# A Hymba-style encoder block: where four streams of elementwise work run, and in which order seven down products are taken

## The chip, the core and the metric

One NeuronCore of a Trainium2 chip runs the kernel. The metric is device time in microseconds, the median of several executions. Five engines have queues of their own, each of which works strictly in the order of the program: TensorE (PE, with its weight loads shown as PEld), VectorE (DVE), ScalarE (ACT), GpSimd (POOL) and SyncE (SP), which issues most of the DMAs. An engine that waits for a semaphore holds up everything behind it in its own queue.

## What is computed

Everything is float32. The input x has 512 rows (tokens) and 2048 columns.

```
h = rmsnorm(x, g_mix)
qA|kA|vA|qB|kB|vB = h @ w_in
out_a = rmsnorm(grouped attention of 8 heads over 2 key/value heads: q, k normalised per head, axial rotary)
out_b = rmsnorm(dilated window attention of 8 heads, partial rotary, three branches merged by softmax weight)
x = x + concat(out_a, out_b) @ w_out
gate, up = split(rmsnorm(x, g_ffn) @ w_gate_up)        # 2 x 5632 columns
x = x + (silu(gate) * up) @ w_down                      # 5632 x 2048
return rmsnorm(x, g_final)
```

## The kernel before

**Split operands.** A matmul here takes operands of a reduced float32 format (fp32r). To keep float32 accuracy each operand is a pair: `hi`, a copy rounded by ACT, and `lo`, the difference `src - hi` made by DVE. A product of two pairs is three matmuls (`mm3`, L133 to L135): hi·hi, hi·lo and lo·hi. So each weight tile of 128 x 1024 that arrives by DMA costs one ACT copy (`split_hi`, L223) and one DVE subtraction (`split_lo`, L231) before the twelve 128x512 matmuls that use it. One such tile with its matmuls is a unit (`Wides`). Its two pairs lie in one of four `twin` buffers.

**Seven products in place of eight.** The large projections use a Strassen-Winograd scheme: a 2x2 block product is made of seven products m1 to m7 of sums of blocks. The sums of weight blocks are made on DVE just before `split_hi` (`weights`, by `tt` at L297 in the projections and L1086 in down). In down (`class Down`, L1056) the weight block `a` of each of 22 row pairs is kept on chip in a `home` buffer. m1 uses a, m7 uses c - b. After that `between` (L1092 to L1095) adds c - b to `home` in place, and m6 (a itself), m4 (d - a) and m5 (c - a) read this new a; m2 uses d, m3 uses c. That in-place sum runs on GpSimd.

**Order of the units.** All units stand in one list that the last loop of the kernel walks. For unit n the loop loads weights some 20 us ahead (`load_raws`), makes `split_hi` up to three units ahead and `split_lo` up to two units ahead (`prepare`), emits the matmuls, runs hooks tied to that unit, and then takes small tasks from two queues `side` and `side2` (`pump`). A unit's `rate` is how many tasks of `side` it takes; `RATE_B`, `RATE_A` and `RATE_2` set this for the attention stage (in units with two halves, eight quarter-rate steps a unit). `drain_until` takes tasks at once where one is needed.

In down the order is written out: m1 leads and m7 follows 8 units behind (`LAG`), so 8 units of m1, then m1 and m7 in turns, then 8 units of m7 alone. Then the same with m6 and m4, and with m5 and m2, and at last m3 alone. m1, m6, m5 and m3 sum into the four PSUM banks called z; m7 and m4 into y, then m2 afresh into y. At the end of m1, m7, m6 and m4, `spill_out` (L1162) copies those four banks to `ev` buffers on ACT (L1167) and GpSimd's queue issues DMAs that add them into a DRAM tensor (L1168); one half of it behind the last unit, the other behind the next. The left operand, activations laid down in DRAM by the gate/up stage, comes in chunks of four row pairs (`chunk`, L1108): a DMA into `form_raw`, an ACT copy (L1119) and a DVE subtraction (L1123).

**The attention stage** runs as `side` tasks beneath the q projections of mixer A and the output projection. Each of 16 heads (`class Head`, L656) takes 12 tasks: transposes and splits of q and k, four `score` and four `weigh` tasks, and, one head later, `pt` (transposes of the probabilities with a split, L711, L124, L125) and `pv`. For a head of mixer B `score` takes the row maximum under a mask on DVE (L696) and at once issues the exponential on ACT (L698); `weigh` takes the reciprocal of its sum and scales the row.

**From attention to gate/up.** `h_side` (L933) turns the normalised rows and makes the block sums of the left operand; for the last column group its `lo` parts are made apart (L953), four of seven on DVE and three on GpSimd. The first gate/up block takes its 28 units in an order written out by hand (`first`, L973), since its last operands are made only then.

Of the kernel before, what the change touches and what calls it, by code (L numbers as in the profile page):

```python
# [14 lines left out]
AF = mybir.ActivationFunctionType  # L15
OP = mybir.AluOpType
# [31 lines left out]
PAIRS = NFF // 2  # L48
LAG = 8
TAIL = 4  # L50
CHUNK = 4
ORDER = ("m1", "m4", "m5", "m3", "m2", "m7", "m6")
X_AT = {"m1": (0, 1), "m4": (0, 2), "m2": (0, 3), "m5": (1, 0), "m6": (1, 1), "m7": (1, 2), "m3": (1, 3)}
RATE_B, RATE_A, RATE_2 = 3.2, 3.2, 3.2


def f32(ap):
    return ap.bitcast(F32)
# [3 lines left out]
def encoder_block(ctx, tc, x, w_in, g_q_a, g_k_a, w_out, w_gate_up, w_down, g_final,  # L62
                  c_xp, c_gain, c_ident, c_mask, c_axial, c_partial, out):
    nc = tc.nc
# [528 lines left out]
    def push_kvA():  # L593
        for t in range(NT):
            push_norm_rope(kvr["t"][:, t, :256], kvr["t"][:, t, :256], t, NKV, "k")

        def turn_k(kv):
            ps = bank("kt")
            for t in range(NT):
                nc.tensor.transpose(ps[:, t * P:(t + 1) * P], kvr["t"][:, t, kv * HD:(kv + 1) * HD], ident)  # L600
            kTA[kv] = split(ps, "kT", None, [kv_split[:, 2 * kv + n] for n in range(2)])

        def split_v():
            vA["v"] = split(kvr["t"][:, :, 256:], "vA", None, [kv_split[:, 4 + 2 * n:6 + 2 * n].rearrange(
                "p a (b c) -> p (a b) c", b=2) for n in range(2)])
        side2.extend((lambda: None, lambda: turn_k(0), split_v, lambda: turn_k(1)))

    q_rows = {}

    def post_qA(j, t, ps):  # L610
        if t == 0:
            q_rows[j] = slot("qA", F32, (P, NT, 512))
        q0 = q_rows[j][:, t]
        nc.scalar.activation(q0, ps[t], AF.Copy, scale=r1["r"][:, t:t + 1])
        push_norm_rope(q0, q0, t, 4, "q")
        side2.append(lambda: qA.__setitem__((j, t), q0))

# [38 lines left out]
    class Head:  # L656
# [27 lines left out]
        def score(self, t):  # L684
            if t == 0:
                self.negm, self.z, self.rz = small(), small(), small()
            ps = bank("sc")
            mm3(ps, cols(self.q, t * P), self.k, True, True)
            p = self.p[t] = slot("p")
            nmx, z = self.negm[:, t:t + 1], self.z[:, t:t + 1]  # L690
            if self.kind == "A":
                nc.vector.tensor_reduce(nmx, ps, axis=AX.X, op=OP.max, negate=True)
                nc.scalar.activation(p, ps, AF.Exp, bias=nmx, accum_out=z)
            else:
                lo = (NT - 1 - t) * P
                nc.vector.tensor_tensor_reduce(p, ps, mask[:, lo:lo + S], -1.0, 3e38, op0=OP.add, op1=OP.min,  # L696
                                               accum_out=nmx)
                nc.scalar.activation(p, p, AF.Exp, bias=nmx, scale=-1.0, accum_out=z)  # L698

        def weigh(self, t):  # L700
            p, rz = self.p[t], self.rz[:, t:t + 1]
# [58 lines left out]
    def push_heads():  # L760
        heads.extend([Head("B", h) for h in range(NHB)] + [Head("A", h) for h in range(NHA)])
        extra = {}
        for g in range(1, NHB // 2):
            h = 2 * g
            extra.setdefault((h - 2, 1), []).append(lambda g=g: load_pair_b(g))
            extra.setdefault((h - 1, 1), []).append(lambda g=g: rope_pair_b(g, "q"))
            extra.setdefault((h - 1, 3), []).append(lambda g=g: rope_pair_b(g, "k"))
            extra.setdefault((h, 1), []).append(lambda g=g: split_pair_v(g))

        def task(n, i):  # L770
            cur = heads[n] if n < len(heads) else None
            prev = heads[n - 1] if 0 < n <= len(heads) else None
            prev2 = heads[n - 2] if n > 1 else None
            t, first = i // 2 - 2, i % 2 == 0
            if t < 0:
                if first:
                    if cur:
                        (cur.tq, cur.tk)[i // 2]()
                else:
                    if prev and i == 1:  # L780
                        prev.weigh(3)
                    if prev2:
                        prev2.pv(2 + i // 2)
                        if i == 3:
                            prev2.fin()
            elif first:
                if prev:
                    if t > 1:
                        prev.pv(t - 2)
                    prev.pt(t)  # L790
            else:
                if cur:
                    cur.score(t)
                    if t:
                        cur.weigh(t - 1)
            for f in extra.get((n, i / 2), ()):
                f()
        for n in range(len(heads) + 1):
            side.extend(lambda n=n, i=i: task(n, i) for i in range(12))
        side.extend(lambda i=i: task(len(heads) + 1, i) for i in (1, 3))  # L800
# [44 lines left out]
    def out_chunk(kind, c):  # L845
# [21 lines left out]
        def post(t):  # L867
            drain_until(lambda: kind in ro, side2)
            nc.vector.scalar_tensor_tensor(x1[c][t], box[t], ro[kind][:, t:t + 1], x1[c][t], op0=OP.mult, op1=OP.add)
            if kind == "A" and c < NC - 1:  # L870
                square_x1(c, t)
            if t < NT - 1:
                return
            if kind == "B":
                hook(now[0] + 1, lambda: park_x1(c))
                return
            if c == 0:
                nc.scalar.activation(slot("table")[:, :1], ones, AF.Silu)
            if c == NC - 1:
                side.extend(lambda p=p: h_side(2 * c, p, True) for p in range(4))  # L880
                side.append(lambda: [square_x1(c, t) for t in (0, 1)])
                side.extend(lambda p=p: h_side(2 * c + 1, p, True) for p in range(2))
                side.append(lambda: park_x1(c))
                side.append(lambda: [square_x1(c, t) for t in (2, 3)])
                side.extend(lambda p=p: h_side(2 * c + 1, p, True) for p in range(2, 4))
                side.append(make_r2)
                return
            for i in (2 * c, 2 * c + 1):
                for part in range(3):
                    side.append(lambda i=i, part=part: h_side(i, part))  # L890
            side.append(lambda: park_x1(c))
# [41 lines left out]
    def h_side(i, half, apart=False):  # L933
# [12 lines left out]
        if half >= 2:  # L946
            for a, lo_part, n in ((0, 1, 4), (1, 5, 3)):
                src = hpart[0][:, lo_part:lo_part + n]
                hi, lo = (arena[a][:, :, i, j] for j in range(2))
                if half == 2:  # L950
                    nc.scalar.activation(hi, src, AF.Copy)
                if half == 3 or not apart:
                    (nc.gpsimd if apart and a else nc.vector).tensor_tensor(lo, src, f32(hi), op=OP.subtract)  # L953
        if half == (3 if apart else 2):
            hf[i] = True

# [13 lines left out]
    def gate_up_block(f0):  # L970
        first = None
        if f0 == 0:
            first = [("m1", 0), ("m1", 1), ("m1", 2), ("m2", 0), ("m2", 1), ("m7", 0), ("m7", 1), ("m1", 3), ("m7", 2),  # L973
                     ("m7", 3)] + [("m6", n) for n in range(4)] + [("m2", 2), ("m2", 3)] \
                + [(f, n) for f in ("m5", "m4", "m3") for n in range(4)]
        box = ColBlock(w_gate_up, 0, (f0 * P, DFF + f0 * P), KD // 4, form_of, 2, first, hf if f0 == 0 else None)
        if f0 == 0:
            for u in units[-len(first):][:10]:
                u.rate, u.load_ahead = 2.0, 10.0
        st = {}  # L980

# [74 lines left out]
    class Down:  # L1056
        BANK = {"m1": "z", "m6": "z", "m5": "z", "m3": "z", "m7": "y", "m4": "y", "m2": "y"}

        def __init__(self):
# [2 lines left out]
            self.home = [down_raw(0, 0, q, "home") for q in range(PAIRS)]  # L1062
            need = {"m1": "", "m7": "bc", "m6": "", "m4": "d", "m5": "c", "m2": "d", "m3": "c"}
            order = []
            for lead, lag in (("m1", "m7"), ("m6", "m4"), ("m5", "m2")):
                for q in range(PAIRS + LAG):
                    if q < PAIRS:
                        order.append((lead, q))
                    if q >= LAG:
                        order.append((lag, q - LAG))  # L1070
            order += [("m3", q) for q in range(PAIRS)]
            self.raws = {}
            for form, q in order:
# [18 lines left out]
        def between(self, form, q):  # L1092
            if form == "m7":
                a = self.home[q].t
                nc.gpsimd.tensor_tensor(a, self.raws[form, q]["b"].t, a, op=OP.add)  # L1095

        def chunks(self):
            uses = {}
# [63 lines left out]
    def spill_out(form, i, j):  # L1162
        def go(t):
            row = 2 * i + t
            for cb in range(2):
                e = evs[turns["ev"] % 2][:, cb]
                nc.scalar.activation(e, box.bank_of(form)[t][cb], AF.Copy, scale=r2["r"][:, row:row + 1])  # L1167
                nc.gpsimd.dma_start(x1_dram[2 * cb + j, row], e, accum_op=OP.add)  # L1168
            turns["ev"] += 1
        for t in range(2):  # L1170
            box.after(form, PAIRS - 1, t, lambda t=t: go(t))

    def add_in(ps, c, t, lo=0, hi=512):
        v = xd[c, t][:, lo:hi]
# [291 lines left out]
```

## Time and profile before

| what | value |
|---|---|
| median of 3 runs | 2009.89 us (2008.53 to 2010.05) |
| the profiled execution: its time / its span | 2010.6 us / 2008.5 us |
| granted TensorE clock, mean | 0.994 |
| busy over the span: PE, DVE, ACT, POOL | 1973.7, 1520.8, 994.2, 278.3 us |
| HBM read / written | 369.65 / 47.45 MB |

The 2.1 us between time and span lie outside the first and last instruction. PE's end times are modelled, so two matmuls that follow closely overlap in the record; the number of matmuls in a stretch tells more than its busy time. Rows of a timeline give start, duration, engine, line, operation, tiles written and read, shapes and count, and in brackets the idle time before and what ended it. Rows by stage give the stage's length, then busy time and number of instructions of PE, PEld, DVE, ACT and POOL, the granted clock, the DMA engines' share and GB/s.

### The profile page before, as it was taken

Reading aid. Unit: us, or ns where it says so; the run is one execution under the profiler, and the core shown is the slowest. Engines: PE = TensorE matmul, PEld = TensorE weight load, DVE = VectorE, ACT = ScalarE, POOL = GpSimd, SP = SyncE. Lnnn points to the kernel's source line nnn. Section 1 sums busy time; section 2 is a strip of 40 time slices with the busy share of each in tenths; the row PEclk is TensorE's granted clock in tenths of the full one; section 3 lists DMA queues with packets and bytes.
Section 4 is the critical chain, followed back from the end, with each engine's and each line's share of the span. In section 5 each row is a group of like instructions: output and inputs, shape, how many; then the busy total and the mean of one; then the engine's idle time right before and its main releaser. Section 6 shows DMA issues by size and latency. Waiting matters only on the chain.

```text
span 2008.5 us, 23826 instructions
## 1 busy us (share of the span) xinstructions
PE 1973.7 (98%) x8932; PEld 1622.4 (81%) x8932; DVE 1520.8 (76%) x1707; ACT 994.2 (49%) x1272; POOL 278.3 (14%) x261
## 2 busy tenths in 40 slices
PE   9999999999999999999999999999999997999998
PEld 7888888778888878888888888888888775888886
DVE  7777757877655687787787777777777999788776
ACT  7654445554435454444444444444544434455464
POOL 3100034663220000000000000000000355002000
PEclk9999999999999999999999999999999998999999
DMA  7777574242245664755856746747659976479855
GB/s 247 261 258 240 183 252 138 95 147 95 96 146 179 215 202 162 266 183 196 270 170 221 260 158 229 229 156 259 196 176 318 338 239 194 152 239 337 283 182 174
DMA packets 219091, 418.67 MB, mean 208 GB/s; under 512 B 13664, under 2 KB 40032, under 8 KB 218720
## 3 DMA queue, kind: packets, MB, share of 16 engines
q1 hardware_dynamic: 210176, 389.86, 58.2%
q0 software_dynamic: 8656, 27.27, 4.4%
q8 instruction: 70, 1.15, 0.2%
q14 instruction: 45, 0.37, 0.1%
q10 hardware_dynamic: 144, 0.02, 0.0%
HBM read 369.65 MB, written 47.45 MB: 208 GB/s over the span
## 4 chain that ended last, share of the span: by engine, by line
PE 89%; DVE 5%; issue 4%; ACT 2%; DMA 1%; POOL 0%; SPq 0%; ACTq 0%; POOLq 0%; DVEq 0%
PE zc L135 10%; PE zc L133 10%; PE zc L134 10%; PE yc L134 5%; PE yc L135 5%; PE yc L133 5%; PE zd L134 3%; PE zd L135 3%; PE zd L133 3%; PE pw L133 3%; PE pw L135 3%; PE pw L134 3%; PE xc L133 2%; PE xc L134 2%; PE xc L135 2%
## 5 line engine op out<-in xcount | busy, mean ns | idle before, releaser
L231 DVE TENSOR_TENSOR twin<-whole,twin 128x1024 fp32r<-128x1024 f32 x172 | 220.8, 1285 | 110.5 <-ACT twin L223 108.1
L223 ACT ACTIVATE twin<-st1b 128x1024 fp32r<-128x1024 f32 x172 | 182.6, 1062 | 214.8 <-PE zc L135 68.7
L133 PE MATMUL zc<-twin,arena 128*128 128x512 f32 x704 | 277.0, 394 | 0.0
L135 PE MATMUL zc<-twin,arena 128*128 128x512 f32 x704 | 274.7, 390 | 0.4 <-DVE arena L953 0.4
L134 PE MATMUL zc<-twin,arena 128*128 128x512 f32 x704 | 274.2, 389 | 0.0
L223 ACT ACTIVATE twin<-whole 128x1024 fp32r<-128x1024 f32 x172 | 181.6, 1057 | 157.5 <-PE yc L135 67.4
L231 DVE TENSOR_TENSOR twin<-st1b,twin 128x1024 fp32r<-128x1024 f32 x172 | 216.0, 1256 | 33.4 <-ACT twin L223 32.7
L223 ACT ACTIVATE twin<-st1a 128x1024 fp32r<-128x1024 f32 x128 | 135.8, 1061 | 192.8 <-PE xc L135 58.2
L231 DVE TENSOR_TENSOR twin<-st1a,twin 128x1024 fp32r<-128x1024 f32 x128 | 171.7, 1342 | 70.0 <-ACT twin L223 60.4
L135 PEld LDWEIGHTS zc<-twin,arena 128*128 128x128 f32 x704 | 132.1, 188 | 28.9 <-DVE arena L953 0.9
L133 PEld LDWEIGHTS zc<-twin,arena 128*128 128x128 f32 x704 | 132.2, 188 | 26.9
L134 PEld LDWEIGHTS zc<-twin,arena 128*128 128x128 f32 x704 | 132.3, 188 | 26.4
L1095 POOL TENSOR_TENSOR home<-st1a,home 128x1024 f32<-128x1024 f32 x8 | 24.5, 3102 | 869.4 <-DMA forms<-pair 855.3
L135 PE MATMUL zd<-twin,form 128*128 128x512 f32 x348 | 136.3, 392 | 5.2 <-DVE form L1123 5.2
L134 PE MATMUL yc<-twin,arena 128*128 128x512 f32 x352 | 137.2, 390 | 1.2 <-DVE twin L231 1.1
L133 PE MATMUL yc<-twin,arena 128*128 128x512 f32 x352 | 138.0, 392 | 0.0
L135 PE MATMUL yc<-twin,arena 128*128 128x512 f32 x352 | 137.2, 390 | 0.0
L134 PE MATMUL zd<-twin,form 128*128 128x512 f32 x348 | 136.0, 391 | 0.1
L133 PE MATMUL zd<-twin,form 128*128 128x512 f32 x348 | 135.9, 391 | 0.0
L134 PE MATMUL yd<-twin,form 128*128 128x512 f32 (+1 forms) x272 | 108.0, 397 | 9.9 <-DVE twin L231 9.9
L135 PE MATMUL yd<-twin,form 128*128 128x512 f32 (+1 forms) x272 | 107.5, 395 | 2.9 <-DVE form L1123 2.9
L133 PE MATMUL yd<-twin,form 128*128 128x512 f32 (+1 forms) x272 | 107.2, 394 | 0.0
(290 smaller groups left out, 4424.4 us busy)
## 6 DMA issues: line engine op xcount, KB each, us to landing
whole<-in_w_gate_up_dram SPq DMA_DIRECT2D x165, 512.0 KB, 5.8
whole<-in_w_in_dram SPq DMA_DIRECT2D x80, 512.0 KB, 4.5
st<-in_w_gate_up_dram SPq DMA_DIRECT2D x55, 512.0 KB, 3.9
st1a<-in_w_down_dram SPq DMA_DIRECT2D x48, 512.0 KB, 6.6
st1b<-in_w_down_dram SPq DMA_DIRECT2D x48, 512.0 KB, 7.5
st1a<-in_w_gate_up_dram SPq DMA_DIRECT2D x44, 512.0 KB, 7.7
st1b<-in_w_gate_up_dram SPq DMA_DIRECT2D x44, 512.0 KB, 7.3
forms<-pair SPq DMA_DIRECT2D x22, 896.0 KB, 6.4
```

Of the source, the lines that this page charges most:

```text
L133: nc.tensor.matmul(dst, ah, bh, start=start, stop=False, skip_group_check=chained)
L134: nc.tensor.matmul(dst, ah, bl, start=False, stop=False, skip_group_check=chained)
L135: nc.tensor.matmul(dst, al, bh, start=False, stop=stop, skip_group_check=chained)
L223: nc.scalar.activation(self.pair[:, :, 0], self.src, AF.Copy)
L231: nc.vector.tensor_tensor(self.pair[:, :, 1], self.src, f32(self.pair[:, :, 0]), op=OP.subtract)
L1095: nc.gpsimd.tensor_tensor(a, self.raws[form, q]["b"].t, a, op=OP.add)
```

## The change

Eight edits stand in the diff. (1) `between` makes the 22 sums into `home` on VectorE. (2) `h_side` makes all its `lo` parts on VectorE. (3) The six products m1, m7, m6, m4, m5, m2 become two queues (m1, m6, m5) and (m7, m4, m2) that take turns without a break; the second starts 8 units later, and a queue that has ended a product lets the other take two units (`PAUSE`) before it starts its next. In the new list m1 takes places 0 to 35, m7 8 to 49, m6 38 to 79, m4 52 to 93, m5 82 to 123, m2 96 to 131; before it was m1 0 to 34, m7 9 to 43, m6 44 to 78, m4 53 to 87, m5 88 to 122, m2 97 to 131. m3 takes 132 to 153 in both. (4) Both halves of `spill_out` hang on the last unit. (5) A score of mixer B leaves its exponential in a list that is emptied at the end of the next task, behind that task's copies. (6) The split of mixer A's values is made in two halves, and empty tasks are put into the side queues. (7) `RATE_A` goes from 3.2 to 3.0. (8) The first gate/up units are reordered.

```diff
+PAUSE = 2
-RATE_B, RATE_A, RATE_2 = 3.2, 3.2, 3.2
+RATE_B, RATE_A, RATE_2 = 3.2, 3.0, 3.2
...
-        def split_v():
-            vA["v"] = split(kvr["t"][:, :, 256:], "vA", None, [kv_split[:, 4 + 2 * n:6 + 2 * n].rearrange(
-                "p a (b c) -> p (a b) c", b=2) for n in range(2)])
-        side2.extend((lambda: None, lambda: turn_k(0), split_v, lambda: turn_k(1)))
+        def split_v(h):
+            vA["v"] = [kv_split[:, 4 + 2 * n:6 + 2 * n].rearrange("p a (b c) -> p (a b) c", b=2) for n in range(2)]
+            split(kvr["t"][:, 2 * h:2 * h + 2, 256:], "vA", None, [w[:, 2 * h:2 * h + 2] for w in vA["v"]])
+        side2.extend((lambda: None, lambda: turn_k(0), lambda: split_v(0), lambda: turn_k(1), lambda: split_v(1)))
...
+        if j and t == 0:
+            side2.extend(4 * [lambda: None])
         push_norm_rope(q0, q0, t, 4, "q")
...
-                nc.scalar.activation(p, p, AF.Exp, bias=nmx, scale=-1.0, accum_out=z)
+                self.late.append(lambda: nc.scalar.activation(p, p, AF.Exp, bias=nmx, scale=-1.0, accum_out=z))
+
+        def flush(self):
+            while self.late:
+                self.late.pop()()
...
+            if first:
+                for h in (prev, cur):
+                    if h:
+                        h.flush()
...
+            side.append(lambda: None)
             for i in (2 * c, 2 * c + 1):
...
-                    (nc.gpsimd if apart and a else nc.vector).tensor_tensor(lo, src, f32(hi), op=OP.subtract)
+                    nc.vector.tensor_tensor(lo, src, f32(hi), op=OP.subtract)
...
-            first = [("m1", 0), ("m1", 1), ("m1", 2), ("m2", 0), ("m2", 1), ("m7", 0), ("m7", 1), ("m1", 3), ("m7", 2),
-                     ("m7", 3)] + [("m6", n) for n in range(4)] + [("m2", 2), ("m2", 3)] \
+            first = [("m1", 0), ("m1", 1), ("m1", 2), ("m2", 0), ("m2", 1), ("m2", 2), ("m7", 0), ("m7", 1), ("m7", 2),
+                     ("m1", 3), ("m7", 3)] + [("m6", n) for n in range(4)] + [("m2", 3)] \
                 + [(f, n) for f in ("m5", "m4", "m3") for n in range(4)]
...
-            for u in units[-len(first):][:10]:
+            for u in units[-len(first):][:11]:
                 u.rate, u.load_ahead = 2.0, 10.0
...
-            for lead, lag in (("m1", "m7"), ("m6", "m4"), ("m5", "m2")):
-                for q in range(PAIRS + LAG):
-                    if q < PAIRS:
-                        order.append((lead, q))
-                    if q >= LAG:
-                        order.append((lag, q - LAG))
+            queues = [deque((f, q) for f in fs for q in range(PAIRS)) for fs in (("m1", "m6", "m5"), ("m7", "m4", "m2"))]
+            hold, turn = [0, LAG], 0
+            while any(queues):
+                if not queues[turn] or hold[turn] > len(order):
+                    turn = 1 - turn
+                order.append(queues[turn].popleft())
+                if order[-1][1] == PAIRS - 1:
+                    hold[turn] = len(order) + PAUSE
+                turn = 1 - turn
             order += [("m3", q) for q in range(PAIRS)]
...
-                nc.gpsimd.tensor_tensor(a, self.raws[form, q]["b"].t, a, op=OP.add)
+                nc.vector.tensor_tensor(a, self.raws[form, q]["b"].t, a, op=OP.add)
...
         for t in range(2):
-            box.after(form, PAIRS - 1, t, lambda t=t: go(t))
+            box.after(form, PAIRS - 1, 0, lambda t=t: go(t))
```

## Prediction

> **What bounds the kernel now.** I read the page first, then the stages, then PE's waits, then the timelines of the engines that PE waits for.
>
> ```profile
> PE 1973.7 (98%) x8932; PEld 1622.4 (81%) x8932; DVE 1520.8 (76%) x1707; ACT 994.2 (49%) x1272; POOL 278.3 (14%) x261
> PE 89%; DVE 5%; issue 4%; ACT 2%; DMA 1%; POOL 0%; SPq 0%; ACTq 0%; POOLq 0%; DVEq 0%
> ```
>
> PE is the bound, and the change removes no matmul. So it can only win where PE stands still or runs slowly. The table by stage shows where that is.
>
> ```profile
> core 0: us, PE busy (x) PEld busy (x) DVE busy (x) ACT busy (x) POOL busy (x), PEclk, DMA share, GB/s
> 300.00:475.00 175.00, 171.02 (x853) 138.55 (x851) 134.17 (x318) 94.00 (x177) 97.43 (x108) 1.00 0.36 117
> 690.00:717.00 27.00, 25.36 (x117) 20.06 (x116) 23.22 (x25) 16.07 (x25) 6.75 (x3) 1.00 0.57 181
> 1575.00:1600.00 25.00, 22.74 (x101) 18.50 (x100) 24.77 (x15) 9.93 (x10) 13.02 (x4) 1.00 1.02 377
> 1600.00:1625.00 25.00, 22.65 (x97) 17.94 (x96) 24.50 (x15) 9.93 (x10) 13.04 (x4) 0.98 0.89 288
> 1575.00:1700.00 125.00, 107.05 (x430) 84.31 (x429) 122.66 (x68) 48.21 (x52) 69.04 (x27) 0.92 0.77 254
> 1700.00:1950.00 250.00, 250.00 (x1104) 207.01 (x1104) 193.27 (x173) 130.20 (x144) 19.29 (x29) 1.00 0.72 239
> ```
>
> Undisturbed down (1700 to 1950) makes 1104 matmuls in 250 us: 0.2264 us each, 2.717 a unit, 5.434 a pair of units. In 1575 to 1700, where m1 and m7 run, 430 matmuls would need 430 x 0.2264 = 97.4 of the 125 us: **27.6 us are lost there**. DVE is busy for 122.66 of the 125. At the start of gate/up 27 - 25.36 = **1.6 us** are lost, in attention 175 - 171.02 = **4.0 us**. These three sums are all that the edits touch. PE's waits in the three stretches, in that order down, gate/up, attention:
>
> ```profile
> PE yd L134 <- DVE twin L231: 9.9, 5, 4.6
> PE zd L135 <- DVE form L1123: 5.2, 3, 2.4
> PE yd L135 <- DVE form L1123: 2.9, 2, 2.3
> ...
> PE yc L134 <- DVE twin L231: 1.1, 1, 1.1
> PE zc L135 <- DVE arena L953: 0.4, 1, 0.4
> ...
> PE pt L711 <- DVE pTl L125: 2.2, 2, 1.1
> PE qt L670 <- POOL qA L577: 0.6, 1, 0.6
> PE pw L133 <- ACT p L693: 0.4, 1, 0.4
> ```
>
> In down the waits sum to 18.0 us, all for DVE. The other 9.6 are clock:
>
> ```profile
> 1619.00:1624.00 5.00, 2.65 (x12) 1.89 (x11) 5.00 (x4) 2.42 (x3) 2.73 (x1) 1.00 0.70 227
> 1624.00:1627.40 3.40, 3.40 (x10) 2.64 (x9) 3.35 (x3) 1.07 (x2) 0.76 (x1) 0.51 0.89 277
> 1668.50:1682.10 13.60, 8.39 (x20) 6.00 (x20) 13.60 (x6) 2.11 (x2) 9.83 (x5) 0.50 0.86 253
> ```
>
> Behind a wait of 2.4 us (the first row idles 5.00 - 2.65) the clock fell to half for 3.4 us, later for 13.6. Why DVE is late is seen in its own timeline and POOL's:
>
> ```profile
> 1575.58 1.21 DVE L1086 TENSOR_TENSOR st1a<-st1a,st1a 128x1024 f32<-128x1024 f32 x1
> 1576.72 1.21 DVE L231 TENSOR_TENSOR twin<-home,twin 128x1024 fp32r<-128x1024 f32 x1
> 1578.01 3.26 DVE L231 TENSOR_TENSOR twin<-st1a,twin 128x1024 fp32r<-128x1024 f32 x1
> 1581.19 1.21 DVE L1086 TENSOR_TENSOR st1b<-st1b,st1b 128x1024 f32<-128x1024 f32 x1
> ...
> 1599.15 1.21 DVE L1123 TENSOR_TENSOR form<-form_raw,form 128x1024 fp32r<-128x1024 f32 x1
> 1623.87 1.21 DVE L1123 TENSOR_TENSOR form<-form_raw,form 128x1024 fp32r<-128x1024 f32 x1
> ...
> 1654.82 1.21 DVE L231 TENSOR_TENSOR twin<-st1b,twin 128x1024 fp32r<-128x1024 f32 x1
> 1655.96 3.41 DVE L1086 TENSOR_TENSOR whole<-whole 128x1024 f32<-128x1024 f32 x1
> 1659.29 1.21 DVE L231 TENSOR_TENSOR twin<-st1b,twin 128x1024 fp32r<-128x1024 f32 x1
> ...
> 1576.93 3.26 POOL L1095 TENSOR_TENSOR home<-st1a,home 128x1024 f32<-128x1024 f32 x1 [4.62 <-DMA form_raw<-forms]
> ```
>
> DVE starts such an operation every 1.14 us (1575.58, 1576.72). But the one that meets a sum on POOL takes until that sum ends: 1578.01 to 1581.19 is 3.18, so 2.04 are blocked. A pair of m1 and m7 costs DVE three operations (3.42), the blocked 2.04, and a half of a form operation (0.57, two in four pairs): 6.03. The form rows confirm it: (1623.87 - 1599.15) / 4 = 6.18. PE needs 5.434. Where m7 runs alone a unit takes DVE 1659.29 - 1654.82 = 4.47 against PE's 2.717.
>
> **Sums on VectorE, and the braid.** The 22 sums leave POOL (3.26 each) and add one operation of 1.14 to DVE, but free it of 2.04. A pair then costs 4 x 1.14 + 0.57 = 5.13, under PE's 5.434. The braid takes away the eight m7 alone, which even without POOL would cost 3.42 + 0.28 = 3.70 against 2.717: they now alternate with m6, which costs one operation, so again 5.13. m5 beside m4 costs four operations too. So DVE keeps up everywhere, at 94%. Its worst eight units are list places 32 to 39: five m7 and three others are 18 operations, with three and a half form chunks 24.5 us against PE's 21.7. DVE falls 2.8 behind and works two units (5.4) ahead, which covers it. Not covered for certain is a delay on ACT just there, since all four copies out of the z banks now stand together:
>
> ```profile
> 1660.44 1.25 ACT L1167 ACTIVATE ev<-zd,whole 128x512 f32<-128x512 f32 x2
> ```
>
> Four are 2.5 us, ahead of the next `split_hi`; DVE's `lo` behind that waits for it. m6's first matmul, and all of PE's queue behind it, waits for the same copies, but the two m7 units between give it 5.4 us; likewise at the ends of m7, m6 and m4. The DMAs that are moved: on SP the two loads of each m7 and the form loads spread over 42 places in place of 35, and on POOL the sixteen adds into DRAM find a queue free of sums, and the reads behind them stay 20 units or more away from the last add. So of the 27.6 I leave about one DVE operation: **-26.5**. Bounds: -27.6 (nothing left) and -14.5, if five bursts of form operations (places 16, 24, 32, 38 and 46) each keep a wait of 2.4 us, as the row of form above has at most, and the one operation is late as well (12.0 + 1.1).
>
> The trace says that the sum costs DVE more on POOL (2.04 blocked) than on DVE itself (1.14). A rule of the Trainium skill points the other way: its page "Perfetto Trace Analysis", section "Optimizing Scalar/DVE Operations", says that with DVE saturated, handing some work to ScalarE or even GPSIMD may make sense. By this rule the stage, with DVE busy 122.66 of 125, would lose by taking the sums back, and the total would be that of the slower rival below; the page adds that the two engines share a port so that it might not help, and the rows side with that.
>
> **The start of gate/up.**
>
> ```profile
> 707.68 2.75 POOL L953 TENSOR_TENSOR arena<-pair,arena 128x768 fp32r<-128x768 f32 x1 [9.50 <-DVE st1b L297]
> 708.66 2.86 DVE L953 TENSOR_TENSOR arena<-pair,arena 128x1024 fp32r<-128x1024 f32 x1
> L953 DVE TENSOR_TENSOR arena<-pair,arena 128x768 fp32r<-128x768 f32 x6 | 5.7, 953 | 0.0
> ```
>
> The same block: 2.86 in place of 1.21. Two such blocks (3.3) go, two operations of 0.95 come: DVE wins 1.4. The new order asks for the last operand two units (5.4 us) later and for each m7's pair one unit later; m2's load goes ahead on SP, m1's back. **-1.4** of the 1.6; bounds -1.6 and +1.1, another wait such as that for `twin`.
>
> **Attention.**
>
> ```profile
> 417.87 0.69 DVE L696 CUSTOM_DVE_ANT_0 p<-sc,btab 128x512 f32<-128x512 f32 x1
> 418.60 0.72 ACT L698 ACTIVATE p<-p,whole 128x512 f32<-128x512 f32 x1 [4.14 <-DVE whole L696]
> 419.32 0.58 ACT L124 ACTIVATE pTh<-pt 128x512 fp32r<-128x512 f32 x1
> 419.93 0.69 DVE L125 TENSOR_TENSOR pTl<-pt,pTh 128x512 fp32r<-128x512 f32 x1 [1.37 <-ACT pTh L124]
> 420.68 0.33 PE L711 MATMUL pt<-whole,p 128*128 128x128 f32 x1 [1.03 <-DVE pTl L125]
> ```
>
> ACT stood 4.14 us at an exponential whose maximum DVE had not made, with the copy `pTh` behind it; DVE and then PE waited. With the exponential behind the copy this chain is gone. The exponentials come one task later; `weigh`, its reciprocal and POOL's scaling follow one task after that, and the transposes that use them a head later: nothing waits. I take both waits for `pTl` (2.2) as gone. The waits for POOL and for a mixer A exponential stay. The halved split moves no work off an engine; empty tasks and `RATE_A` move 6 of some 206 tasks (16 units x 8 steps x 0.05) past the first half of the output projection, at three a unit two units late, a unit before the last head is wanted. **-2.2**; bounds -4.0 (all) and +2.2 (as much new).
>
> **Sum.** 26.5 + 1.4 + 2.2 = 30.1 off the profiled execution's 2010.6 (span 2008.5 and 2.1 around it) is 1980.5. It ran 0.7 above the median 2009.89, so the median becomes **1979.8 us**.
>
> **Rivals.**
> *DVE stays the bound in the braid*: at 94% bursts are not regained. Four pairs have 21.7 us for 18 operations, so this decides from a spacing of 1.21, the rows' own duration. It costs the 13.1 of the bound in place of 1.1: 1979.8 + 12.0 = 1991.8. For: DVE is busy 24.77 of 25 now. Against: the 1.14 spacing. 10%.
> *DMA becomes the bound*: a pair needs three tiles and half a form tile of 128x1024 f32, 3.5 x 0.524 = 1.835 MB; in 5.434 us that is 338 GB/s for 14 pairs. The row at 1600 moved 288 at a share of 0.89, 324 at full: 5.66 a pair, 14 x 0.23 = 3.2 us, 1983.0. Against: 377 in the row before. 8%.
> *Attention gives back*: the later exponentials and tasks put in new waits, +2.2 in place of -2.2: 1984.2. 8%.
> *Slower*: the long DVE rows are not blocked by POOL but slow by themselves, so the 22 sums only add 22 x 1.14 = 25.1 to an engine that sets the pace: with the other two terms 2009.9 + 25.1 - 3.6 = 2031.4. It decides if DVE's 3.2 us rows remain with POOL empty. Against: the long row ends one operation after POOL's (1581.27 and 1580.19). 3%.
> *No change*: the lost time is handed to another wait in down, such as m6's for the z banks. 2%.
> The forecast has 69%.
>
> A measurement of this kernel can tell about 0.2%, 4 us. All but the last two cases are faster by more: 0.95 faster, 0.02 within, 0.03 slower. The range takes in the lower bounds (2009.9 - 27.6 - 1.6 - 4.0 = 1976.7, less the 1.5 by which the three runs shown differ, 1975.2) and the first rival (1991.8): 1975.2 to 1991.8.
>
> **What would show it.** Right: in the stage of m1 and m7 some 110 matmuls in each 25 us, clock 1.00, no POOL rows from `between`, DVE rows of 1.21 alone at some 94%; no wait for `pTl` in attention. Wrong: DVE rows over 3 us, PE waits for `twin` or `form` at each chunk, a DMA wait ahead of L1086, or PE's first m6 matmul behind ACT's L1167.

## The result and the profile after

The changed kernel takes 1974.46 us (median of 4 runs, 1974.26 to 1974.71) against 2009.7 us for the kernel before (4 runs, 2008.53 to 2010.05): a ratio of 0.9826, 95% interval 0.9809 to 0.9843. It is faster by 35.2 us where 30.1 were forecast, and the time lies 0.7 below the lower end of the range.

The page of the kernel after, and its table by stage with the stages of before (columns as there):

```profile
span 1972.9 us, 23779 instructions
PE 1959.5 (99%) x8932; PEld 1618.4 (82%) x8932; DVE 1501.2 (76%) x1732; ACT 995.0 (50%) x1273; POOL 211.4 (11%) x237
PE 96%; DVE 1%; DMA 1%; ACT 1%; issue 0%; POOL 0%; ACTq 0%; POOLq 0%; SPq 0%
```

```profile
300.00:475.00 175.00, 173.75 (x876) 143.31 (x875) 142.60 (x321) 95.72 (x181) 99.55 (x106) 1.00 0.37 122
690.00:717.00 27.00, 27.00 (x125) 22.34 (x124) 26.11 (x29) 18.17 (x28) 1.91 (x1) 1.00 0.62 214
1575.00:1600.00 25.00, 25.00 (x112) 20.72 (x111) 25.00 (x23) 12.53 (x12) 0.00 (x0) 1.00 1.05 390
1600.00:1625.00 25.00, 25.00 (x112) 20.69 (x112) 23.61 (x21) 12.21 (x12) 0.00 (x0) 1.00 0.98 361
1575.00:1700.00 125.00, 125.00 (x553) 103.55 (x552) 114.88 (x101) 64.20 (x67) 7.14 (x8) 1.00 0.83 278
```

PE made 430 matmuls between 1575 and 1700; now it makes 553 (46 units in place of 36), without a gap and at full clock. DVE does 101 operations there in place of 68 and is busy for less time, though other units lie in these 125 us now. All that PE waits for from the attention stage on is this:

```profile
PE o L134 <- DVE pTl L126: 1.0, 1, 1.0
PE pw L134 <- DVE pTl L126: 0.3, 1, 0.3
```

Both waits are in attention and for `pTl`, where I had said that none would be left; the waits for POOL and for an exponential of mixer A, which I had said would stay, are gone.

The braid in DVE's timeline (L1101 makes c - b, L1110 the sum into home, L1138 a form chunk):

```profile
1586.21 1.22 DVE L1138 TENSOR_TENSOR form<-form_raw,form 128x1024 fp32r<-128x1024 f32 x1
1587.35 1.22 DVE L1110 TENSOR_TENSOR home<-whole,home 128x1024 f32<-128x1024 f32 x1
1588.48 1.22 DVE L232 TENSOR_TENSOR twin<-whole,twin 128x1024 fp32r<-128x1024 f32 x1
1589.62 1.22 DVE L1101 TENSOR_TENSOR st1a<-st1a,st1a 128x1024 f32<-128x1024 f32 x1
1590.75 1.22 DVE L232 TENSOR_TENSOR twin<-home,twin 128x1024 fp32r<-128x1024 f32 x1
```

Every operation starts 1.13 to 1.14 us after the one in front; the rows of 3 us are gone.

Where the 35.6 us of the spans come from is read from the starts of four matmuls in PE's timeline: the first of a score, the first of gate/up (`zc` from `arena`), the first of down (`zd`) and the last. The first score starts 0.11 us earlier than before. From start to start:

| stretch | before | after | difference | forecast |
|---|---|---|---|---|
| first score to gate/up | 403.95 | 399.14 | -4.81 | -2.2 |
| gate/up to down | 862.02 | 859.25 | -2.77 | -1.4 |
| down to the last matmul | 449.18 | 421.23 | -27.95 | -26.5 |

### The profile page after: what moved, and what is told of

It reads as the page before. It is cut to its first block, busy times and chain, and to the rows that moved or that the text cites. A ratio compares the mean times of both kernels' runs of the same rounds, so it can differ in the third digit from the quotient of the medians.

```text
span 1972.9 us, 23779 instructions
## 1 busy us (share of the span) xinstructions
PE 1959.5 (99%) x8932; PEld 1618.4 (82%) x8932; DVE 1501.2 (76%) x1732; ACT 995.0 (50%) x1273; POOL 211.4 (11%) x237
## 4 chain that ended last, share of the span: by engine, by line
PE 96%; DVE 1%; DMA 1%; ACT 1%; issue 0%; POOL 0%; ACTq 0%; POOLq 0%; SPq 0%
PE zc L136 10%; PE zc L134 10%; PE zc L135 10%; PE yc L136 5%; PE yc L134 5%; PE yc L135 5%; PE zd L135 4%; PE zd L136 4%; PE zd L134 4%; PE yd L134 3%; PE yd L135 3%; PE yd L136 3%; PE pw L134 3%; PE pw L136 3%; PE pw L135 3%; PE xc L136 3%
## 5 line engine op out<-in xcount | busy, mean ns | idle before, releaser
L232 DVE TENSOR_TENSOR twin<-whole,twin 128x1024 fp32r<-128x1024 f32 x172 | 216.7, 1262 | 105.5 <-ACT twin L224 105.5
L134 PE MATMUL zc<-twin,arena 128*128 128x512 f32 x704 | 277.3, 394 | 0.0
L232 DVE TENSOR_TENSOR twin<-st1b,twin 128x1024 fp32r<-128x1024 f32 x172 | 210.2, 1222 | 37.7 <-ACT twin L224 36.0
L232 DVE TENSOR_TENSOR twin<-st1a,twin 128x1024 fp32r<-128x1024 f32 x128 | 156.5, 1223 | 68.6 <-ACT twin L224 61.0
L134 PEld LDWEIGHTS zc<-twin,arena 128*128 128x128 f32 x704 | 132.3, 188 | 26.9
L134 PE MATMUL yc<-twin,arena 128*128 128x512 f32 x352 | 138.1, 392 | 0.0
L134 PE MATMUL zd<-twin,form 128*128 128x512 f32 x348 | 135.7, 390 | 0.0
L1183 POOL DMA_DIRECT2D x1d<-ev x16 | 14.2, 1098 | 1086.0 <-DMA form_raw<-forms 939.1
L134 PE MATMUL yd<-twin,form 128*128 128x512 f32 (+1 forms) x272 | 105.1, 386 | 0.0
L135 PE MATMUL yd<-twin,form 128*128 128x512 f32 (+1 forms) x272 | 105.1, 386 | 0.0
L136 PE MATMUL yd<-twin,form 128*128 128x512 f32 (+1 forms) x272 | 105.1, 386 | 0.0
```

The lines of the kernel that those rows point to most:

```text
L134: nc.tensor.matmul(dst, ah, bh, start=start, stop=False, skip_group_check=chained)
L135: nc.tensor.matmul(dst, ah, bl, start=False, stop=False, skip_group_check=chained)
L136: nc.tensor.matmul(dst, al, bh, start=False, stop=stop, skip_group_check=chained)
L232: nc.vector.tensor_tensor(self.pair[:, :, 1], self.src, f32(self.pair[:, :, 0]), op=OP.subtract)
```

## Experiments

The stretches of this table are used below as well, since kernels that differ only behind the first score start it anywhere from 282.8 to 284.1 us, so the time ahead of it says nothing of the change. In runs whose edit lies in another stretch, the three repeat within 0.1, 0.2 and 0.1 us. My theory in down is that the sums (blocked by POOL) and the order (m7 alone) are two causes that add up, but for what DVE's work ahead absorbs. The rivals are that one of them did it all.

**Sums on GpSimd again, braid kept.**

```diff
-                nc.vector.tensor_tensor(a, self.raws[form, q]["b"].t, a, op=OP.add)
+                nc.gpsimd.tensor_tensor(a, self.raws[form, q]["b"].t, a, op=OP.add)
```

> The changed kernel with one edit undone: the 22 sums into home run on GpSimd again, the braid stays. My theory, that the blocked time on DVE is a cause of its own: DVE needs 6.03 to 6.18 us a pair against PE's 5.434, over 22 pairs 13 to 16 us behind, less the 5.4 us that it works ahead, plus a few us of half clock: 8 to 16 us above the changed kernel's 1974.5, so 1982 to 1990, with DVE rows over 3 us in the braid. The rival, that the braid alone did it, because only m7 by itself overran DVE: at most 2 us, 1974 to 1977.

Measured: 1991.95 us (1990.64 to 1992.29). Down takes 438.82, 17.6 more. DVE's timeline and PE's waits in down:

```profile
1590.46 1.21 DVE L232 TENSOR_TENSOR twin<-home,twin 128x1024 fp32r<-128x1024 f32 x1
1591.59 3.38 DVE L1138 TENSOR_TENSOR form<-form_raw,form 128x1024 fp32r<-128x1024 f32 x1
1594.90 1.21 DVE L232 TENSOR_TENSOR twin<-whole,twin 128x1024 fp32r<-128x1024 f32 x1
```

```profile
PE zd L136 <- DVE form L1138: 9.3, 6, 2.6
PE zd L135 <- DVE twin L232: 1.4, 1, 1.4
PE yd L135 <- DVE twin L232: 0.6, 2, 0.3
```

The braid alone does not do it. The accounts gave 22 pairs x (6.18 - 5.434) = 16.4, less the 5.4 of work ahead, 11.0. The rows of the waits sum to 11.3, but that is not like for like: of the 17.6, 3.4 are two stretches of half clock and the other 14.2 are waits, 2.9 of which their rows do not show (below). So the accounts were some 3 us short, and the median is 2.0 above my range.

**The old order of the products, sums on DVE.**

```diff
-            queues = [deque((f, q) for f in fs for q in range(PAIRS)) for fs in (("m1", "m6", "m5"), ("m7", "m4", "m2"))]
...
+            for lead, lag in (("m1", "m7"), ("m6", "m4"), ("m5", "m2")):
+                for q in range(PAIRS + LAG):
...
```

> The changed kernel with the down products in the order of before (m7 alone for its last eight units), the sums on DVE. My theory, that the braid is a cause of its own: m7 alone costs DVE 3.70 against PE's 2.717, 7.9 us over eight units, less the 5.4 that it works ahead: 2.5, with a stretch of half clock up to 4.2: 1977 to 1979, the wait at the end of m7, and no DVE row over 1.3 us. The rival, that taking the sums off POOL alone did it: under 1 us, 1974 to 1975.5.

Measured: 1976.57 us (1976.24 to 1976.91); down takes 423.77, 2.54 more. PE's waits in down:

```profile
PE yd L135 <- DVE twin L232: 1.4, 3, 0.8
```

The 2.5 us that m7 alone was to cost are there, no clock is lost, and no row of DVE in down is longer than 1.23 us. The median is 0.4 below the range that I gave, since that added some half clock. So in down: as before 449.18, braid alone 438.82 (-10.4), sums alone 423.77 (-25.4), both 421.23 (-28.0). The two overlap (10.4 and 25.4 are more than 28.0), and taking the sums off POOL is by far the larger cause. Edit (4), the copies out of the banks, stands in the last three of these four and was not undone by itself; no such copy is among PE's waits in the kernel before or in the changed one.

**No pause between the products of a queue.**

```diff
-PAUSE = 2
+PAUSE = 0
```

> The changed kernel with PAUSE at 0: each product of a queue starts at once in its turn, so one unit (2.7 us) lies between the last matmul into a set of PSUM banks and the next product's first one, in place of two or three. The four copies take 2.5 us on ACT and can be behind one other operation of 1.06. If PE's wait for these copies is the next limit: some 0.5 to 1.5 us at each of the ends of m1, m7, m6 and m4, 2 to 5 us, 1976.5 to 1979.5, with PE waits for ACT's ev copies in down. If ACT is fast enough even so: within 0.4 us of 1974.5.

Measured: 1974.61 us (1973.84 to 1975.12), down 421.28: no difference. No copy out of the banks shows among PE's waits. ACT's timeline at the end of m1 shows why:

```profile
1639.61 0.67 ACT L1182 ACTIVATE ev<-zd,whole 128x512 f32<-128x512 f32 x1
1640.63 1.85 ACT L1182 ACTIVATE ev<-zd,whole 128x512 f32<-128x512 f32 x3 [0.35 <-PE zd L136]
1642.36 1.06 ACT L224 ACTIVATE twin<-home 128x1024 fp32r<-128x1024 f32 x1
```

The first copy starts at 1639.61, while m1's last unit still runs on the other banks (its last matmul starts at 1640.89), and all four are done at 1642.48. m6's first matmul comes at 1643.83. The pauses are a reserve that this kernel does not need.

**The first gate/up units in the old order, all lo parts on DVE.**

```diff
-            first = [("m1", 0), ("m1", 1), ("m1", 2), ("m2", 0), ("m2", 1), ("m2", 2), ("m7", 0), ("m7", 1), ("m7", 2),
-                     ("m1", 3), ("m7", 3)] + [("m6", n) for n in range(4)] + [("m2", 3)] \
+            first = [("m1", 0), ("m1", 1), ("m1", 2), ("m2", 0), ("m2", 1), ("m7", 0), ("m7", 1), ("m1", 3), ("m7", 2),
+                     ("m7", 3)] + [("m6", n) for n in range(4)] + [("m2", 2), ("m2", 3)] \
...
-            for u in units[-len(first):][:11]:
+            for u in units[-len(first):][:10]:
```

> The changed kernel with the first gate/up units in the order of before, all lo parts still on VectorE. My theory, that the lock was the smaller part and the order the larger: of the 2.8 us that this stage won some 1 to 1.5 are lost, 1975.5 to 1976. The rival, that taking the two operations off POOL did it all (DVE wins 1.4 and the wait for the twin pair was 1.1): under 0.4 us.

Measured: 1975.8 us (1975.32 to 1976.15); gate/up 860.24, +1.0.

**The last lo parts on GpSimd again, the new order kept.**

```diff
-                    nc.vector.tensor_tensor(lo, src, f32(hi), op=OP.subtract)
+                    (nc.gpsimd if apart and a else nc.vector).tensor_tensor(lo, src, f32(hi), op=OP.subtract)
```

> The changed kernel with the last column group's three lo parts on GpSimd again, the first gate/up units in the new order. If the order alone covers DVE's delay (the last operand is wanted 5.4 us later and each m7 pair one unit later): under 0.4 us above 1974.5. If DVE's 3.3 us under the lock decide: 1 to 1.5 us, 1975.5 to 1976, with a wait for a twin pair on PE near 700.

Measured: 1974.94 us (1974.73 to 1975.75), between my two forecasts; gate/up 860.04, +0.8. PE's waits from 680 to 720, first the old order, then the lo parts on GpSimd:

```profile
PE yc L135 <- DVE twin L232: 0.7, 1, 0.7
```

```profile
PE yc L135 <- DVE twin L232: 0.4, 1, 0.4
```

Of the 2.77 won here each edit alone leaves a wait of the same kind, for a `twin` pair; neither did it alone, and neither covers the other. The order's share is somewhat larger, as I held, but the difference between the two is within what such runs can tell.

**Exponentials at once.**

```diff
-                self.late.append(lambda: nc.scalar.activation(p, p, AF.Exp, bias=nmx, scale=-1.0, accum_out=z))
+                nc.scalar.activation(p, p, AF.Exp, bias=nmx, scale=-1.0, accum_out=z)
```

> The changed kernel with mixer B's exponentials issued at once, as before. My theory, that ACT's stand at the exponentials made PE wait: both waits for pTl come back, 2.2 to 3 us above 1974.5, 1976.5 to 1977.5. The rival, that the other edits in the attention stage (the halved split, the empty tasks, RATE_A) removed the waits by shifting tasks against each other: under 1 us, 1974 to 1975.5.

Measured: 1981.11 us (1980.9 to 1981.49), 6.6 above the changed kernel, three times what I expected; the attention stretch takes 405.75, 1.8 more than in the kernel before. PE's waits from 300 to 450 in this run:

```profile
PE pt L718 <- DVE p L711: 2.3, 2, 1.2
PE sc L134 <- DVE pTl L126: 1.5, 4, 0.6
PE qt L673 <- POOL qA L578: 0.8, 1, 0.8
PE pt L718 <- DVE pTl L126: 0.4, 1, 0.4
PE kt L601 <- POOL kvr L578: 0.3, 1, 0.3
```

ACT's waits for DVE's maximum there, in the kernel before and in this run, and then the longest waits of all engines in the changed kernel:

```profile
ACT p L698 <- DVE whole L696: 42.1, 22, 4.1
```

```profile
ACT p L701 <- DVE whole L699: 47.5, 24, 5.3
```

```profile
ACT pTh L125 <- PE pt L718: 27.3, 20, 3.0
...
ACT p L701 <- DVE whole L699: 6.0, 6, 1.5
```

ACT stood 47.5 us at exponentials that waited for DVE's maximum, and only 6.0 with them behind the copies, where it mostly waits for PE's transposes. Other waits than those for `pTl` come back as well, so the late exponentials take away more than the one chain that I had followed. That another attention edit costs time when the exponentials are early called for more runs.

**The late exponentials alone, in the kernel before.**

```diff
-                nc.scalar.activation(p, p, AF.Exp, bias=nmx, scale=-1.0, accum_out=z)
+                self.late.append(lambda: nc.scalar.activation(p, p, AF.Exp, bias=nmx, scale=-1.0, accum_out=z))
...
+            if first:
+                for h in (prev, cur):
+                    if h:
+                        h.flush()
```

> The kernel before with one edit alone: mixer B's exponentials issued behind the next task's copies. From the first score to the first gate/up matmul the kernel before took 403.95 us, the changed one 399.14, the changed one with early exponentials 405.75. If the attention edits simply add, this edit alone wins 6.6 us: 397.3 in that stretch, 2003.1 in all. My theory, that it removes the waits behind ACT's stand at the exponentials and that the slower rate then takes away a loss that only appears with the late exponentials (2.0 with RATE_A at 3.2 in the changed kernel): it wins 2 to 4 us, 400 to 402 in that stretch, 2005.5 to 2007.5.

Measured: 2006.36 us (2003.52 to 2007.3), a ratio of 0.998 (0.997 to 0.999); the attention stretch takes 400.26, -3.7. That is what I expected and not the 6.6 of a sum: the edits don't simply add.

**RATE_A back at 3.2.**

```diff
-RATE_B, RATE_A, RATE_2 = 3.2, 3.0, 3.2
+RATE_B, RATE_A, RATE_2 = 3.2, 3.2, 3.2
```

> The changed kernel with RATE_A at 3.2. The last six tasks of the heads go back into the first half of the output projection. Matmuls stay the same in number, so it should cost nothing unless a wait for an exponential of mixer A comes back (0.4 in the trace of before): 1974.3 to 1975. The rival, that the slower rate won part of the 4.8 us of attention: 0.5 to 1.5 us, 1975 to 1976.

Measured: 1976.74 us (1976.61 to 1977.06); the attention stretch 401.10, +2.0. The rival was right, and with more than the 0.5 to 1.5 that it had. PE in 475 to 525: the kernel before, the changed one, this one, and the one with late exponentials alone (rate 3.2 too):

```profile
475.00:525.00 50.00, 50.00 (x246) 41.01 (x245) 35.24 (x59) 23.56 (x48) 15.61 (x15) 1.00 0.37 120
```

```profile
475.00:525.00 50.00, 50.00 (x248) 41.29 (x246) 32.78 (x59) 24.80 (x48) 18.21 (x16) 1.00 0.41 134
```

```profile
475.00:525.00 50.00, 48.97 (x238) 39.60 (x237) 34.57 (x65) 24.04 (x47) 17.61 (x16) 1.00 0.40 131
```

```profile
475.00:525.00 50.00, 49.48 (x241) 40.25 (x240) 32.63 (x56) 24.12 (x47) 14.56 (x13) 1.00 0.40 132
```

Rate 3.2 shows no loss with early exponentials (x246) and seven to ten matmuls fewer, some 2 us, with late ones. PE's waits from 470 to 530 in this run, none of which the changed kernel has:

```profile
PE pw L134 <- ACT p L696: 0.7, 1, 0.7
PE pw L134 <- DVE xrows L880: 0.3, 1, 0.3
```

So PE stands behind an exponential of mixer A and behind DVE's work on `xrows`. Why these come late at this rate was not settled.

**Mixer A's values split in one piece; no empty tasks.** Two kernels, each with one of these changes from the changed kernel.

```diff
-        side2.extend((lambda: None, lambda: turn_k(0), lambda: split_v(0), lambda: turn_k(1), lambda: split_v(1)))
+        side2.extend((lambda: None, lambda: turn_k(0), split_v, lambda: turn_k(1)))
```

```diff
-        if j and t == 0:
-            side2.extend(4 * [lambda: None])
...
-            side.append(lambda: None)
             for i in (2 * c, 2 * c + 1):
```

> The changed kernel with mixer A's values split in one piece, as before. If the one long operation on DVE (1.78 us under the lock in the trace of before, ahead of the copy for pTl) was a cause of its own: 0.5 to 1.3 us, one wait for pTl near 380, 1975 to 1976. If the late exponentials had already taken that wait away: under 0.3 us.

> The changed kernel without its empty tasks (four before the second group of q rows of mixer A, one before each h_side group). If they part the DVE work of the q rows from the scores: 0.3 to 1 us above 1974.5 in 400 to 440, and 0.1 in the second half of the output projection. If they only shift where tasks fall: within 0.3 us either way.

Measured: 1973.91 us (1973.26 to 1974.46) and 1974.57 (1974.35 to 1974.69); the attention stretch takes 398.61 and 399.40. The halved split does not win but lose 0.5 us: in one piece the wait for `pTl` of 1.0 in the changed kernel is 0.2 (`PE o L134 <- DVE pTl L126: 0.2, 1, 0.2`). The empty tasks win 0.3 in the stretch and nothing that the medians show. The kernel with the split in one piece is the fastest of all that ran, by 0.03%, which such a measurement can't tell from no difference.

**The same two with early exponentials.** The last two runs ask which edit cost 1.8 us there; each has one of the two diffs above and the one of the exponentials at once.

> The changed kernel with early exponentials (as in the run that gave 1981.11) and mixer A's values split in one piece. With early exponentials the attention stretch took 405.75 us, 1.8 more than the kernel before, so one of the other attention edits costs time there. If it is the halved split, which the changed kernel also does 0.5 better without: 1.5 to 2.5 us less, 403 to 404.3 in the stretch, 1978.5 to 1979.8. If not: 405.2 to 406.2.

> The changed kernel with early exponentials and without the empty tasks. If the empty tasks are what costs 1.8 us with early exponentials, because they crowd the q rows of mixer A behind them: 403 to 404.3 us in the attention stretch, 1978.5 to 1979.8. If not: 405.2 to 406.2, 1980.6 to 1981.6.

Measured: 1978.99 us (1978.38 to 1979.97) and 1981.86 (1981.27 to 1982.55); stretches of 403.37 and 406.58. It is the halved split: without it the stretch falls by 2.4, below that of the kernel before. The empty tasks win 0.8 here.

## Why the prediction was wrong

*The kind of change was right, and the largest term.* DVE's spacing is 1.14 with POOL empty, a braided pair fits, and down won 27.95 where I said 26.5; the two experiments in down bear out both causes (14.2 lost in waits where 11.0 were worked out; 2.5 for m7 alone, as worked out). I left 1.1 us for a delay behind the four copies on ACT; they delayed nobody, even without a pause. DVE is full from 1575 to 1600 (25.00 of 25), and the work ahead covered it.

*The step that failed is the size of what there was to win outside down.* I wrote "at the start of gate/up 27 - 25.36 = 1.6 us are lost, in attention 175 - 171.02 = 4.0 us" and that "these three sums are all that the edits touch". In down I had counted matmuls; in the other two stages I subtracted PE's busy time. The stretches show 2.77 and 4.81 won, more than I allowed to be there. Busy time hides part of each wait, because the records of two matmuls overlap. The kernel before, at one wait of gate/up:

```profile
712.62 0.39 PE L133 MATMUL yc<-twin,arena 128*128 128x512 f32 x1
714.13 0.50 PE L134 MATMUL yc<-twin,arena 128*128 128x512 f32 x1 [1.13 <-DVE twin L231]
714.47 0.40 PE L135 MATMUL yc<-twin,arena 128*128 128x512 f32 x1
```

The wait's row says 1.13. From start to start it is 1.51 where 0.227 is usual: 1.28 lost. The next matmul starts 0.34 later, again 0.11 too many. So 1.39 us are lost at a wait of 1.13, a quarter of a microsecond more at each. The two other short waits of that stage cost 0.71 and 0.34 by the same reading, so the three cost 2.4 where their rows sum to 1.6. In attention the rows of eight waits sum to the 4.0; from start to start they cost 5.3, without the matmul behind each. So both ceilings were too low, and with them the lower end of the range, which was made of the three ceilings. The same reading was wrong in down, without harm to the sum: beside 18.0 of waits I called the other 9.6 clock. PE was busy 3.40, 8.39 and 2.80 us in the three stretches at half clock, which lost half of that, 7.3; the other 2.3 belong to the waits.

*Two sizes in attention were wrong for reasons of their own.* I gave the late exponentials 2.2 and RATE_A, the halved split and the empty tasks nothing. Alone the exponentials won 3.7. With them the slower rate is worth 2.0, which I had taken as a pure shift of six tasks because I only asked when the last head is wanted, not what else runs in the stage from which they are moved. The halved split loses 0.5 and leaves most of the wait for `pTl` that is still there. I had followed a single chain of waits (ACT at 418.60) and taken the total of PE's waits for one tile as the gain, though ACT stood 42 us in the same way all along the stage.

*The rivals.* "DVE stays the bound" and "slower" fell with the timeline above: 1.14 a step, no row over 1.23 us. "DMA becomes the bound" fell too: 390 and 361 GB/s were moved in the two windows of the braid where I needed 338, and no load stands among PE's waits. "Attention gives back" holds for the halved split alone, with 0.5 of the 4.4 us. "No change" fell with the time: no wait for the z banks came, even without a pause.

## What to carry to other kernels

An operation that is moved to an idle engine can cost the busy one more than it saves: compare the blocked time beside it (2.04 us here) with its price at home (1.14). Put work that overruns an engine beside work that does not, so that each pair fits, and give up an order with a run of the dear kind alone. Read what can be won in a stage from starts or counts of matmuls, not from PE's busy time, and undo small edits one by one: of the edits here one lost time, and one was worth something only beside another.

## What the runs showed of the hardware

The clock gate can be read closely. Between the first and the last change, all stretches of half and of full clock in the records of these runs last a multiple of 3.41 us (3.41, 10.24, 13.65 and 40.96 in the kernel before), so there is a grid. PE's busy time in windows of that grid, first in the kernel before, then with the sums on GpSimd:

```profile
1596.78:1600.19 3.41, 2.05 (x9) 1.70 (x10) 3.41 (x3) 0.00 (x0) 0.22 (x1) 1.00 0.81 272
1620.67:1624.08 3.41, 1.21 (x5) 1.03 (x6) 3.41 (x3) 0.75 (x1) 1.06 (x1) 1.00 0.53 157
1624.08:1627.49 3.41, 3.41 (x9) 2.65 (x9) 3.34 (x4) 1.16 (x2) 0.85 (x1) 0.50 0.90 282
1665.04:1668.45 3.41, 1.60 (x7) 0.92 (x5) 3.41 (x3) 1.06 (x1) 1.63 (x2) 1.00 1.01 247
1668.45:1671.86 3.41, 2.81 (x7) 2.12 (x7) 3.41 (x3) 1.06 (x1) 1.95 (x2) 0.50 1.10 256
```

```profile
1593.46:1596.87 3.41, 1.84 (x8) 1.54 (x9) 3.41 (x3) 0.00 (x0) 0.43 (x1) 1.00 1.00 325
1617.35:1620.76 3.41, 1.02 (x4) 0.86 (x5) 3.41 (x3) 0.02 (x1) 1.25 (x1) 1.00 0.92 306
1620.76:1624.17 3.41, 3.41 (x9) 2.63 (x8) 3.34 (x4) 1.58 (x2) 2.08 (x1) 0.50 0.95 329
```

Waits of 2.3 to 2.6 us that fell into one window (1.21 and 1.02 busy) were followed by a window at half clock; waits of the same size that lay across a border (2.05 and 1.84 busy) were not. The Trainium skill, on the page "TensorE: Matmul & The Clock Gate", section "Why this matters for your kernels", asks for no idle gap over about 3 us; the trace shows that 2.4 us can be enough, by where they fall. What decides by these rows is the busy share of a window. In the traces of all fourteen kernels every window of the grid at full clock with at most 1.61 us busy (eight in down, the others at a kernel's end) was followed by half clock, and every one with 1.83 or more by full clock; so the cut, if it is one, lies between these, by PE's records with their modelled ends.
